# A residual tail without turns between blocks, and rows turned by transposition in place of a product with a diagonal, at the end of an attention layer

## The chip, the core and the metric

The kernel runs on one core of a Trainium2 chip. The metric is the device time of one execution in microseconds; a kernel's time is the median of its runs. The core's engines work from queues of their own, each in its program's order: TensorE (PE; its weight loads are listed as PEld), VectorE (DVE), ScalarE (ACT), GpSimd (POOL) and SyncE (SP), which here issues the transfers (DMAs).

## What is computed

The reference is one step of a two-layer decoder trunk over 1024 prompt rows and 8 x 4 sample rows of width 1024, in float32. The first layer is sliding-window attention (16 heads of 64, 4 key heads), the second a gated DeltaNet (16 value heads of 128, a short causal convolution, chunks solved one after another). In short:

```
for layer in (attention, DeltaNet):
    shift, scale, gate = split(silu(c) @ w_mod[layer] + b_mod[layer], 3)
    h = rms_norm(x, norm_g[layer]) * (1 + scale) + shift
    x = x + gate * branch(h)          # branch = (mixer(h) * silu(z)) @ w_out
y = rms_norm(x, final_norm_g)
```

The change lies where the first layer ends and the second begins: `x + gate * branch(h)` for the attention layer, and `rms_norm`, `scale` and `shift` for the DeltaNet layer.

## The kernel before

**Numbers.** A product of float32 matrices is made of three faster ones: each operand is split into a rounded part (`hi`, type fp32r) and a rest (`lo`), and hi x hi, hi x lo and lo x hi are summed in PSUM. Rows are worked in nine blocks: eight of 128 prompt rows and one of the 32 sample rows. The output projection of layer 1 takes them in the order of `turned_` (L1136), which is 0, 8, 1, 2, ..., 7. The text calls the position in this list the block's place: place 1 is the sample block (t = 8), place 8 the last full block (t = 7).

**How the order is made.** While the program is written out, the class `Core` (L96 to L175) keeps a table of assumed durations: for each engine the time at which it would be free, for each tile the time at which it would be written. Work beside the main line of matmuls stands in generators, which `weave` (L486) puts into a list sorted by a rank from the table `K` (L241). Between two matmuls of the main line, `stages` (L497) goes through the list and advances each generator as far as its condition lets it: `ready` (the tiles are written by TensorE's assumed time), `soon`, `idle` (an engine is about to be free), or a counter. So the order of every engine's queue is fixed before the kernel runs, and on the chip an instruction that is late holds up everything behind it on its engine. `until` (L508) holds the main line itself until a condition is met.

**Around the change.** The loop at L1437 takes the places 0 to 8. For each it does 48 matmuls into two PSUM banks, one for each half (512 columns, `hf`) of the output row; `opened` counts the banks that are not yet read. When a half is complete it weaves `add_out` (L1337). For a full block that is: wait for its turn; multiply the bank by `gate` into a tile `y` (VectorE), which closes the bank; add `y` to the row block `xt` (GpSimd; at place 8, second half, VectorE); square with a row sum (ScalarE). With the second half the row block is stored to `x1d` and `shape` is woven (L1376): the row sum becomes rs = 1/sqrt(mean + eps) by some 13 small VectorE steps (`rsqrt`, L196); VectorE makes `dg`, the identity times rs; for each half of the block TensorE multiplies four 128 x 128 pieces of `xt` with `dg`, which scales the rows and turns them at once; the result is scaled and shifted (ScalarE for the first half, VectorE for the second) into `fu`, and split into `h2hi` (ScalarE) and `h2lo` (VectorE). Then `shaped` goes up by one.

The turn of an addition is this condition in `add_out` (L1341), for place i and half hf:

```
yield lambda: gathered[0] == 2 * i + hf and i in rows_ and shaped[0] >= i - 1 + hf
```

that is: the additions come in order, the row block has been asked for, and so many blocks are shaped. `rows_in` (L1328) asks for the row block of place i once `shaped[0] >= i - 1`, into a ring of two tiles. `y` and `dg` share another ring of two.

**What follows.** At place 7 `first_weights` (L1420) is woven; once the gate of layer 2 is computed it loads and splits the convolution's weights `cwr` (turned into `cT`) and the first key weights `kw0`, `kw1`. Behind the projection, `run_k` (L2147) starts the first key projection of layer 2, in groups of 384, 384 and 288 rows of h2: group 0 waits until at most one bank is in `opened`, group 1 until none is (L2149). The first query projection follows with its groups 0 and 1, then the 288-wide groups of both. A group of h2 is used once 4, 7 or 9 blocks are shaped (L556). `decays` (L1502), woven too, multiplies h2 with the small weights `wab` by the same groups, and then computes the decay of each head by a long chain of VectorE and ScalarE steps; TensorE sums its result `gpr` at L1586. `projector` (L576) loads the weights of the next projections (`wr`), and splits them on ScalarE (`wh`) and GpSimd (`wl`). `conv` (L1655) copies a projection to `XR` and applies the taps of the convolution.

In the profile all operations of this part carry the line L89, that of the helper which records them, so they are told apart by the names of their tiles.

Of the kernel before, what the change touches and what calls it, by code (L numbers as in the profile page):

```python
# [5 lines left out]
F32 = mybir.dt.float32  # L6
F32R = mybir.dt.float32r
I32 = mybir.dt.int32
AF = mybir.ActivationFunctionType
# [5 lines left out]
P = 128  # L15
D = 1024
# [175 lines left out]
def f(ap):  # L192
    return ap.bitcast(F32)
# [26 lines left out]
def body(tc, I, O, cst_ap, dbg=None):  # L220
    nc = tc.nc
# [25 lines left out]
    SEQ = [(a[0], int(a[1:])) for a in """z0 z1 z2 k1 v0 q1 z3 v1 k2 q2 z4 z5 k3 v2 q3 z6 z7 k4 v3 q4 z8 z9 k5 v4 q5  # L247
        z10 z11 k6 v5 q6 z12 z13 k7 v6 q7 v7 z14 z15""".split()]
    MM = (0, 20)
    ORDER = [("q", 2), ("q", 3), ("q", 4), ("q", 5), ("z", 0), ("k", 1), ("z", 1), ("z", 2), ("q", 6), ("q", 7),  # L250
             ("z", 3), ("z", 4), ("z", 5), ("z", 6), ("z", 7)]
    SE = ("vector", "vector", "vector", "vector")
# [44 lines left out]
    ident = C["ident"]  # L297
# [220 lines left out]
    def plain():  # L518
        return not isinstance(nc, Core)

    def ready(*ts):
        return lambda: plain() or nc.ready(ts) <= nc.free["tensor"]
# [4 lines left out]
    def idle(eng, *ts):  # L527
        return lambda: plain() or max(nc.free[eng], nc.ready(ts)) <= nc.free["tensor"] + AI
# [7 lines left out]
    def bank(tag):  # L536

        q = held.setdefault(tag, [])
        yield lambda: len(q) < banks[tag] or q[-banks[tag]] is None
        t = psb(tag)  # L540
        q.append(t.tensor.name)
        yield lambda: plain() or nc.after(nc.used, t, "tensor") <= nc.free["tensor"]
        return t
# [80 lines left out]
    for t in range(NB + 1):  # L624
        parts = P if t < NB else TS
# [62 lines left out]
    def qpieces(pr, g):  # L688
        return [(64 * a, ((2 * pr + a) * 4 + g) * 64, 64) for a in range(2)]
# [73 lines left out]
    if True:  # L763
# [373 lines left out]
        split_, gathered, placed = {}, [-1], set()  # L1137
# [81 lines left out]
        for m in range(KD // 2):  # L1219
# [7 lines left out]
        plan = [(win, {"k": lambda b: [(0, 1024 + b * P, P)], "q": lambda b: qpieces(b // 4, b % 4), "z": zpieces}[a](b))  # L1227
                for a, b in ORDER]
        w_raw, w_split, projected = projector(plan)
# [3 lines left out]
        for t in range(NB + 1):  # L1233
            parts = P if t < NB else TS
            pv = psb("pj3")[0:parts, 0:256]
            n = 0
            for k in range(KD):
                hi, lo = wv[k // 2]
                for x, y in ((hhi, hi), (hlo, hi), (hhi, lo)):
                    with pinned():  # L1240
                        mm = nc.tensor.matmul(pv, x[:, k, t * P:t * P + parts], y[:, k % 2, :],
                                              start=(n == 0), stop=(n == 23))
# [7 lines left out]
        pt = psb()  # L1250
# [5 lines left out]
        def modulation_rest():  # L1256
# [12 lines left out]
            for k in range(KD):  # L1269
                yield lambda: ticks[0] >= t0 + MM[0] + MM[1] * (2 * k + 1)  # L1270
                yield ready(*wts)
# [16 lines left out]
        nc = Core(tc)  # L1288
# [8 lines left out]
        weave(keys0[0], "turning")  # L1297
        for i, (a, b) in enumerate(ORDER):
            if a == "k":
# [12 lines left out]
    if True:  # L1312
# [9 lines left out]
        x2 = Watched(nc, x2_guard.__enter__(), since=nc.free["tensor"])  # L1322
        nc.parts.add(x1d.tensor.name)
        gate = x2.tile([P, D], F32, name="gp")
        rows_, opened, outs, shaped = {}, [], [0], [0]
        kwr, kw = [], []

        def rows_in(i, t):  # L1328
            yield lambda: shaped[0] >= i - 1
            xt = rows_[i] = x2.tile([P, D], F32, tag="xt", name="xt", bufs=2)  # L1330
            nc.sync.dma_start(xt[0:P if t < NB else TS], xp_rows[t * P:(t + 1) * P] if t < NB else xs_rows)
            if t == NB:
                o, w = COFF["sels"]
                selt = rows_["sel"] = xo.tile([P, w], F32, name="sels")
                nc.sync.dma_start(selt, cst_ap[:, o:o + w])

        def add_out(pj, i, t, hf):  # L1337

            parts = P if t < NB else TS
            ns = slice(hf * 512, (hf + 1) * 512)  # L1340
            yield lambda: gathered[0] == 2 * i + hf and i in rows_ and shaped[0] >= i - 1 + hf  # L1341
            xt = rows_[i][0:parts]
            if t < NB:
                yield idle("vector", pj)
                y = x2.tile([P, 512], F32, tag="y", name="y", bufs=2)
                nc.vector.tensor_tensor(y, pj, gate[:, ns], ALU.mult)
                opened.pop(0)
            else:
                yield idle("scalar", pj)
                y = x2.tile([P, 512], F32, tag="y", name="y", bufs=2)  # L1350
                nc.scalar.copy(y[0:TS], pj[TS:2 * TS])
                yield idle("vector", y)
                nc.vector.tensor_tensor(y[0:TS], y[0:TS], pj[0:TS], ALU.add)
                opened.pop(0)
                selt = rows_["sel"]
                yield ready(selt)
                pg = yield from bank("lg")
                nc.tensor.matmul(pg[0:TS], selt[:, hf * TS:(hf + 1) * TS], modGt, start=True, stop=True)
                yield idle("vector", y, pg)
                nc.vector.tensor_tensor(y[0:TS], y[0:TS], pg[0:TS], ALU.mult)  # L1360
                give("lg", pg)
            eng = "vector" if i == NB and hf else "gpsimd"
            yield idle(eng, y, xt)
            getattr(nc, eng).tensor_tensor(xt[:, ns], xt[:, ns], y[0:parts], ALU.add)
            if hf == 0:
                rows_["ss", i] = sm.tile([P, 2], F32, tag="ss", name="ss")[0:parts]
            yield soon(xt)
            nc.scalar.activation(y[0:parts], xt[:, ns], AF.Square, accum_out=rows_["ss", i][:, hf:hf + 1])
            gathered[0] += 1
            if hf == 1:  # L1370
                nc.sync.dma_start(x1d[t * P:t * P + parts], xt)
                weave(shape(i, t, xt, rows_["ss", i], parts), "shape")
                if t == NB:
                    weave(modulation_gate(1, wp, 4, "wr"), "mod")

        def shape(i, t, xt, ss, parts):  # L1376

            nonlocal x2_guard
            yield idle("vector", ss)
            sv = sm.tile([P, 1], F32, tag="sv", name="sv")[0:parts]  # L1380
            nc.vector.tensor_tensor(sv, ss[:, 0:1], ss[:, 1:2], ALU.add)
            nc.vector.tensor_scalar(sv, sv, 1.0 / D, EPS, ALU.mult, ALU.add)
            rs = sm.tile([P, 1], F32, tag="rs", name="rs")[0:parts]
            rsqrt(nc, sm, rs, sv, 1, parts)
            dg = x2.tile([P, 512], F32, tag="y", name="dg", bufs=2)[0:parts, 0:parts]
            nc.vector.tensor_scalar_mul(dg, ident[0:parts, 0:parts], rs)
            for kk in range(2):
                yield ready(dg, xt)
                pt = yield from bank("lg")
                for q in range(4):  # L1390
                    nc.tensor.matmul(pt[:, q * parts:(q + 1) * parts], xt[:, (4 * kk + q) * P:(4 * kk + q + 1) * P], dg,
                                     start=True, stop=True)
                fu = x2.tile([P, 4, P], F32, tag="fu", name="fu", bufs=2)
                yield soon(pt, fu)
                for q in range(4):
                    k = 4 * kk + q
                    if t < NB and kk == 0:
                        nc.scalar.activation(fu[:, q, :], pt[:, q * P:(q + 1) * P], AF.Identity,
                                             bias=Sh[1][:, k, 0:1], scale=Sc[1][:, k, 0:1])
                    elif t < NB:  # L1400
                        nc.vector.tensor_scalar(fu[:, q, :], pt[:, q * P:(q + 1) * P],
                                                Sc[1][:, k, 0:1], Sh[1][:, k, 0:1], ALU.mult, ALU.add)
                    else:
                        o3 = fu[:, q, 0:TS].rearrange("p (b t) -> p b t", t=DS)
                        nc.vector.tensor_tensor(o3, pt[:, q * TS:(q + 1) * TS].rearrange("p (b t) -> p b t", t=DS),
                                                Sc[1][:, k, 1:9].unsqueeze(2).to_broadcast([P, DB, DS]), ALU.mult)
                        nc.vector.tensor_tensor(o3, o3, Sh[1][:, k, 1:9].unsqueeze(2).to_broadcast([P, DB, DS]), ALU.add)
                give("lg", pt)
                fv = fu[:, :, 0:parts]
                c0 = t * P % GW  # L1410
                hi, lo = (h[t // 3][:, 4 * kk:4 * kk + 4, c0:c0 + parts] for h in (h2hi, h2lo))
                yield idle("scalar", fu)
                nc.scalar.copy(hi, fv)
                yield idle("vector", hi)
                nc.vector.tensor_sub(lo, fv, f(hi))
            shaped[0] += 1
            if shaped[0] == NB + 1:
                x2_guard.__exit__(None, None, None)
# [18 lines left out]
        for i, t in enumerate(turned_):  # L1437
# [7 lines left out]
            for kk, hf in order if i < NB else sorted(order, key=lambda o: o[::-1]):  # L1445
                if True:
                    ns = slice(hf * 512, (hf + 1) * 512)
                    if hf not in pjs:
                        tag = ("pj", "pj", "mi", "mi")[outs[0] % 4]
# [5 lines left out]
                    for k in range(4 * kk, 4 * kk + 4):  # L1455
# [187 lines left out]
    if True:  # L1643
# [544 lines left out]
        pos, prepared, stored, opened, gathered, outs = [0], {}, [0], [], [-1], [0]  # L2188
# [485 lines left out]
    nc = nc.nc  # L2674
# [36 lines left out]
```

## Time and profile before

| | us |
|---|---|
| median of three runs | 1722.98 |
| lowest and highest run | 1719.68, 1724.67 |
| the profiled execution | 1721.68 |
| its span in the profile | 1719.9 |
| output projection of layer 1, first to last matmul of places 0 to 8, in the trace | to 535.3 |
| last row block shaped (last `h2lo`) | 569.2 to 569.9 |

Times in the trace count from the span's start. A row of a timeline has the start, the duration, engine, line, operation, output<-inputs, shape and count, and in brackets how long the engine had been idle and what it waited for. Matmuls overlap, so the distance of two starts, not the duration, says what one costs.

### The profile page before, as it was taken

Reading aid. Unit: us, or ns where it says so; the run is one execution under the profiler, and the core shown is the slowest. Engines: PE = TensorE matmul, PEld = TensorE weight load, DVE = VectorE, ACT = ScalarE, POOL = GpSimd, SP = SyncE. Lnnn points to the kernel's source line nnn. Section 1 sums busy time; section 2 is a strip of 40 time slices with the busy share of each in tenths; the row PEclk is TensorE's granted clock in tenths of the full one; section 3 lists DMA queues with packets and bytes.
Section 4 is the critical chain, followed back from the end, with each engine's and each line's share of the span. In section 5 each row is a group of like instructions: output and inputs, shape, how many; then the busy total and the mean of one; then the engine's idle time right before and its main releaser. Section 6 shows DMA issues by size and latency. Waiting matters only on the chain.

```text
span 1719.9 us, 31798 instructions
## 1 busy us (share of the span) xinstructions
PE 1629.0 (95%) x10666; PEld 1436.5 (84%) x10666; DVE 1204.6 (70%) x3538; ACT 862.6 (50%) x2514; POOL 613.4 (36%) x1170
## 2 busy tenths in 40 slices
PE   6999999998999999999899999999999998999897
PEld 5988888986777898999889899899999896767685
DVE  4526676564565578897889878788797875468677
ACT  4625565444333546475463655654656654333332
POOL 2601111112112226463453534445344455323332
PEclk9999999999999999999999999999999999999999
DMA  9542221233243142232332324224242237765885
GB/s 331 150 138 66 59 58 50 56 89 111 86 134 105 54 111 50 66 97 56 106 74 66 98 52 112 64 72 114 51 115 60 51 85 209 236 181 160 255 259 171
DMA packets 281573, 191.78 MB, mean 112 GB/s; under 512 B 98361, under 2 KB 253881, under 8 KB 281378
## 3 DMA queue, kind: packets, MB, share of 16 engines
q1 hardware_dynamic: 281410, 189.75, 38.1%
q8 instruction: 85, 1.39, 0.3%
q14 instruction: 78, 0.64, 0.1%
HBM read 144.68 MB, written 47.04 MB: 111 GB/s over the span
## 4 chain that ended last, share of the span: by engine, by line
PE 30%; DVE 8%; DMA 4%; ACT 3%; issue 2%; POOL 2%; SPq 1%; POOLq 0%; ACTq 0%; DVEq 0%
PE ps_pj L89 17%; PE ps_lg L89 4%; PE ps_mi L89 4%; PE ps_tr L89 2%; PE ps_ob L89 2%; DMA S<-in_state_gdn_s 2%; DVE vT L89 1%; DVE UZ L89 1%; DMA out_new_s_s<-S 1%; POOL rst L89 1%; DMA out_y_p<-xt 1%; DVE rst L89 1%; DVE S L89 1%; SPq L89 1%; DVE tmp L89 0%
## 5 line engine op out<-in xcount | busy, mean ns | idle before, releaser
L89 PE MATMUL ps_pj<-h2hi,wl 128*128 128x384 f32 (+1 forms) x1128 | 383.1, 340 | 2.7 <-POOL wl L89 2.7
L89 PE MATMUL ps_pj<-h2hi,wh 128*128 128x384 f32 (+1 forms) x1128 | 383.2, 340 | 2.1 <-ACT wh L89 2.1
L89 PE MATMUL ps_pj<-h2lo,wh 128*128 128x384 f32 (+1 forms) x1128 | 381.6, 338 | 0.0
L89 POOL TENSOR_TENSOR wl<-wr,wh 128x512 fp32r<-128x512 f32 x122 | 163.4, 1340 | 543.3 <-ACT wh L89 492.9
L89 PEld LDWEIGHTS ps_pj<-h2hi,wl 128*128 128x128 f32 x1128 | 216.0, 191 | 6.8 <-POOL wl L89 3.6
L89 PEld LDWEIGHTS ps_pj<-h2hi,wh 128*128 128x128 f32 x1128 | 215.9, 191 | 4.8 <-ACT wh L89 2.4
L89 PEld LDWEIGHTS ps_pj<-h2lo,wh 128*128 128x128 f32 x1128 | 215.7, 191 | 3.3
L89 POOL TENSOR_TENSOR xt<-xt,y 128x512 f32<-128x512 f32 (+1 forms) x48 | 64.0, 1337 | 173.5 <-DVE y L89 138.1
L89 PE MATMUL ps_pj<-hlo,wh 128*128 128x384 f32 (+1 forms) x360 | 119.0, 331 | 0.0
L89 PE MATMUL ps_pj<-hhi,wh 128*128 128x384 f32 (+1 forms) x360 | 118.4, 329 | 0.0
L89 PE MATMUL ps_pj<-hhi,wl 128*128 128x384 f32 (+1 forms) x360 | 117.9, 328 | 0.0
L89 DVE SCALAR_TENSOR_TENSOR vT<-XR,cT,vT 128x384 f32<-128x384 f32 (+1 forms) x144 | 90.5, 638 | 25.4 <-ACT vT L89 23.8
L89 DVE TENSOR_TENSOR X<-X,tmp 64x31 f32<-64x31 f32 (+15 forms) x248 | 95.2, 384 | 8.5
L89 DVE TENSOR_TENSOR tmp<-X 64x31 f32<-64x31 f32 (+15 forms) x248 | 93.5, 377 | 4.9 <-POOL X L89 1.7
L89 ACT CAST wh<-wr 128x512 fp32r<-128x512 f32 x122 | 75.1, 616 | 13.1 <-PE ps_pj L89 8.0
L89 PEld LDWEIGHTS ps_pj<-hlo,wh 128*128 128x128 f32 x360 | 67.7, 188 | 11.2 <-issue 11.1
L89 ACT ACTIVATE vo<-vo,fo 128x128 f32<-128x128 f32 x128 | 42.2, 392 | 59.7 <-POOL fo L89 59.7
L89 PEld LDWEIGHTS ps_pj<-hhi,wh 128*128 128x128 f32 x360 | 67.7, 188 | 2.7 <-issue 2.7
L89 ACT ACTIVATE prob<-prob,nm 128x256 f32<-128x256 f32 (+1 forms) x128 | 62.2, 489 | 14.8 <-DVE nm L89 14.6
L89 PEld LDWEIGHTS ps_pj<-hhi,wl 128*128 128x128 f32 x360 | 67.7, 188 | 2.1 <-issue 2.1
L89 POOL TENSOR_TENSOR Xd<-Xc,cst 32x128 f32<-32x128 f32 x128 | 65.7, 513 | 10.7 <-DMA Xc<-Xdd 3.1
L89 ACT ACTIVATE qe<-ps_mi,Eg 128x128 f32<-128x128 f32 x112 | 35.0, 363 | 64.4 <-PE ps_mi L89 64.4
(580 smaller groups left out, 4235.0 us busy)
## 6 DMA issues: line engine op xcount, KB each, us to landing
wr<-in_gdn_w_in SPq DMA_DIRECT2D x96, 256.0 KB
S<-in_state_gdn_s SPq DMA_DIRECT2D x40, 256.0 KB
xt<-in_x_prompt SPq DMA_DIRECT2D x16, 512.0 KB
wm<-in_w_mod SPq DMA_DIRECT2D x16, 512.0 KB
wr<-in_swa_w_in SPq DMA_DIRECT2D x64, 128.0 KB
wmod<-in_w_mod SPq DMA_DIRECT2D x32, 256.0 KB
wm<-in_w_mod SPq DMA_DIRECT2D x32, 256.0 KB
DP<-gcr SPq DMA_DIRECT2D x64, 128.0 KB
```

What stands on the lines that cost most here:

```text
L89: inst = fn(*args, **kwargs)
```

## The change

Three things are edited. In `add_out` the part of the condition that counts shaped blocks is dropped; the order of the additions, and the row block being asked for, stay. `rows_in` gets a name, XT, for the size of its ring and for the condition that goes with it; with XT = 2 it is what it was. And `shape` has a second way of turning, used at the places in TP2: it scales each half of the row block by rs into a tile `xs` of its own, the first half on VectorE, the second on ScalarE (TE2), and turns the four pieces by transpositions. TP2 holds 0 to 7, so this is done for seven full blocks and the sample block; place 8 keeps the product with `dg`, which gets a ring of its own.

```diff
+    TP2, TE2 = (0, 1, 2, 3, 4, 5, 6, 7), ('vector', 'scalar')
+    XT = 2
...
         def rows_in(i, t):
-            yield lambda: shaped[0] >= i - 1
-            xt = rows_[i] = x2.tile([P, D], F32, tag="xt", name="xt", bufs=2)
+            yield lambda: shaped[0] >= i - XT + 1
+            xt = rows_[i] = x2.tile([P, D], F32, tag="xt", name="xt", bufs=XT)
...
-            yield lambda: gathered[0] == 2 * i + hf and i in rows_ and shaped[0] >= i - 1 + hf
+            yield lambda: gathered[0] == 2 * i + hf and i in rows_
...
-            dg = x2.tile([P, 512], F32, tag="y", name="dg", bufs=2)[0:parts, 0:parts]
-            nc.vector.tensor_scalar_mul(dg, ident[0:parts, 0:parts], rs)
+            plain_ = i in TP2
+            if not plain_:
+                dg = x2.tile([P, P], F32, tag="dg", name="dg", bufs=2)[0:parts, 0:parts]
+                nc.vector.tensor_scalar_mul(dg, ident[0:parts, 0:parts], rs)
             for kk in range(2):
+                if plain_:
+                    xs = x2.tile([P, 512], F32, tag="xs", name="xs", bufs=2)[0:parts]
+                    eng = TE2[kk]
+                    yield idle(eng, rs)
+                    if eng == "scalar":
+                        nc.scalar.activation(xs, xt[:, kk * 512:(kk + 1) * 512], AF.Copy, scale=rs)
+                    else:
+                        getattr(nc, eng).tensor_scalar_mul(xs, xt[:, kk * 512:(kk + 1) * 512], rs)
+                    yield ready(xs)
+                    pt = yield from bank("lg")
+                    for q in range(4):
+                        nc.tensor.transpose(pt[:, q * parts:(q + 1) * parts], xs[:, q * P:(q + 1) * P],
+                                            ident[0:parts, 0:parts])
+                else:
...
```

More of the change, by code (lines that the diff above doesn't have):

```diff
@@ L1384, in shape @@
             rsqrt(nc, sm, rs, sv, 1, parts)
-            dg = x2.tile([P, 512], F32, tag="y", name="dg", bufs=2)[0:parts, 0:parts]
-            nc.vector.tensor_scalar_mul(dg, ident[0:parts, 0:parts], rs)
+            plain_ = i in TP2
+            if not plain_:
+                dg = x2.tile([P, P], F32, tag="dg", name="dg", bufs=2)[0:parts, 0:parts]
+                nc.vector.tensor_scalar_mul(dg, ident[0:parts, 0:parts], rs)
             for kk in range(2):
[L1388 to L1392, printed above, removed]
+                if plain_:
[12 more added lines that the diff above has]
+                else:
+                    yield ready(dg, xt)
+                    pt = yield from bank("lg")
+                    for q in range(4):
+                        nc.tensor.matmul(pt[:, q * parts:(q + 1) * parts], xt[:, (4 * kk + q) * P:(4 * kk + q + 1) * P], dg,
+                                         start=True, stop=True)
                 fu = x2.tile([P, 4, P], F32, tag="fu", name="fu", bufs=2)
```

## The prediction

> **What bounds the kernel now.** I read the page's totals, then busy time by stretches around the output projection of layer 1 (the code the change touches), then TensorE's waits there, then the timelines of TensorE, VectorE and GpSimd.
>
> ```profile
> span 1719.9 us, 31798 instructions
> PE 1629.0 (95%) x10666; PEld 1436.5 (84%) x10666; DVE 1204.6 (70%) x3538; ACT 862.6 (50%) x2514; POOL 613.4 (36%) x1170
> ```
> ```profile
> 200.00:300.00 100.00, 100.00 (x690) 86.85 (x686) 69.11 (x254) 57.87 (x190) 11.69 (x9) 1.00 0.21 57
> ...
> 430.00:530.00 100.00, 100.00 (x500) 76.99 (x499) 59.52 (x184) 36.45 (x85) 19.84 (x15) 1.00 0.32 106
> ...
> 530.00:540.00 10.00, 6.71 (x34) 4.74 (x27) 7.66 (x18) 4.41 (x9) 7.29 (x9) 0.94 0.71 190
> 540.00:550.00 10.00, 10.00 (x50) 9.33 (x50) 2.06 (x5) 2.51 (x8) 1.53 (x3) 0.72 0.34 95
> 580.00:590.00 10.00, 6.75 (x42) 6.25 (x41) 9.23 (x21) 4.22 (x10) 5.48 (x10) 1.00 0.21 55
> 590.00:600.00 10.00, 10.00 (x60) 9.82 (x59) 3.48 (x12) 5.68 (x17) 2.90 (x9) 0.83 0.42 119
> 600.00:610.00 10.00, 7.53 (x27) 6.70 (x26) 6.75 (x24) 5.36 (x20) 2.51 (x2) 0.68 0.67 177
> ```
> ```profile
> PE ps_lg L89 <- DVE gpr L89: 3.2, 1, 3.2
> PE ps_lg L89 <- DVE cT L89: 3.0, 1, 3.0
> PE ps_pj L89 <- ACT wh L89: 2.1, 1, 2.1
> PE ps_pj L89 <- ACT XR L89: 0.8, 1, 0.8
> ...
> PE ps_lg L89 <- DVE dg L89: 0.3, 1, 0.3
> ```
>
> The columns of a stretch are its length, then busy time of PE, PEld, DVE, ACT and POOL, the granted TensorE clock, the DMA share and GB/s. From 430 to 530, while the nine blocks go through the output projection, TensorE is busy 100.00 of 100.00 at clock 1.00; VectorE has 40 us free, ScalarE 64. So here TensorE's own work sets the time: whatever its queue loses is won, and work given to VectorE or ScalarE is covered. Behind 530 this ends. The waits of TensorE between 430 and 620 (waiter, releaser, total, times, longest) are four of weight, and after three of them the granted clock is below one: 0.72 in 540 to 550, 0.83 in 590 to 600, 0.68 in 600 to 610. A wait there costs its own length and then about (1 - clock) of the next 10 us.
>
> **Turning by transposition.** Now each half of a normalised block is turned by four plain matmuls of a block of rows with diag(rs).
>
> ```profile
> L89 PE MATMUL ps_lg<-dg,xt x144: 270/275/579, 438.2 to 564.6; 128*128 128x128 f32 x128, 32*128 32x32 f32 x16
> ```
> ```profile
> 467.48 0.39 PE L89 MATMUL ps_mi<-wlo,ohi 128*128 128x512 f32 x1
> 467.71 1.05 PE L89 MATMUL ps_lg<-dg,xt 128*128 128x128 f32 x8
> 468.52 0.48 PE L89 MATMUL ps_pj<-whi,ohi 128*128 128x512 f32 x1
> 468.83 0.40 PE L89 MATMUL ps_pj<-whi,olo 128*128 128x512 f32 x1
> ...
> 453.27 1.07 PE L89 MATMUL ps_lg<-dg,xt 32*128 32x32 f32 x8
> ...
> 454.61 0.40 PE L89 MATMUL ps_mi<-whi,olo 128*128 128x512 f32 x1
> ...
> 598.97 0.60 PE L89 MATMUL ps_mi<-cst,kT 128*128 128x128 f32 x4
> ...
> 599.60 0.34 PE L89 MATMUL ps_pj<-h2lo,wh 128*128 128x384 f32 x1
> 599.78 0.34 PE L89 MATMUL ps_pj<-h2hi,wl 128*128 128x384 f32 x1
> ```
>
> Nine blocks of two halves of four are 72 matmuls with 144 records: a plain float32 matmul leaves two. Starts, not durations, give the price, since matmuls overlap. From the burst at 467.71 to the second matmul behind it are 1.12 us; the one projection matmul in between takes 0.23 (467.48 to 467.71), so a burst costs 0.89. The sample block's (32 rows) costs 454.61 - 453.27 - 0.23 = 1.11. Four float32 transpositions stand in the trace as four records, at 598.97: 599.60 - 598.97 less one matmul of 0.18 is 0.45. A full half saves 0.44. The sample block's transposition by the new code has no row; it is no dearer than 0.45 and no cheaper than nothing, so it saves 0.66 to 1.11; I take 0.66.
>
> TP2 holds the places 0 to 7 in the order 0, 8, 1, ..., 7 of `turned_`: the sample block is in it, the last full block (place 8) is not and keeps the diagonal. Places 0 and 2 to 6 are turned before the projection ends: 12 halves x 0.44 + 2 x 0.66 = 6.6 us off a TensorE without a gap. Place 7 falls into the tail, where TensorE waits anyway; I count nothing for it.
>
> What it adds:
>
> ```profile
> L89 DVE TENSOR_SCALAR dg<-cst,rs x9: 228/287/1600, 436.3 to 559.6; 128x128 f32<-128x128 f32 x8, 32x32 f32<-32x32 f32 x1
> ```
> ```profile
> L89 DVE TENSOR_SCALAR prob<-prob,sm x128: 276/348/1427, 120.8 to 372.0; 128x256 f32<-128x256 f32 x112, 128x128 f32<-128x128 f32 x16
> ```
> ```profile
> L89 ACT ACTIVATE y<-xt x18: 622/632/643, 430.8 to 556.1; 128x512 f32<-128x512 f32 x16, 32x512 f32<-32x512 f32 x2
> ```
> ```profile
> 474.72 0.69 DVE L89 TENSOR_TENSOR h2lo<-fu,h2hi 128x512 fp32r<-128x512 f32 x1 [0.69 <-ACT h2hi L89]
> 475.33 0.68 DVE L89 TENSOR_TENSOR y<-ps_mi,gp 128x512 f32<-128x512 f32 x1
> ```
>
> VectorE scales a 128x512 half in place of making a 128x128 diagonal. The same operation took 0.29 at 128 columns and 0.35 at 256, 0.06 more; carried on that is 0.47 at 512, and the 0.68 of a two-operand 512 bounds it above: 0.2 to 0.4 more, eight times, at most 3.2 us of 40 free. ScalarE gets eight new 128x512 scalings, 0.63 each by its square of that size: 5.1 us of 64 free. Both cost the end nothing while TensorE is full. Uncovered (a row split `ohi` queued behind a scaling in ScalarE's order, with TensorE waiting for it) a scaling would cost up to 0.63, all eight 5.1.
>
> In front of this row a rule speaks against the edit. The Trainium skill, "TensorE: Matmul & The Clock Gate", Part 4, gives about 275 ns for a transposition in a kernel, and says that transpose mode does not count as busy for the clock. By that price four would take 1.1 us, an estimate from the page. The trace agrees with the duration of a record (0.60 for four overlapped) but not with adding them; and 200 to 300, where attention turns its probabilities by transposition all the time, kept clock 1.00.
>
> **The looser turns.** `add_out` waited for `shaped[0] >= i - 1 + hf`. For the first half `rows_in` still asks for the same number (XT is 2), so nothing changes. For the second half the wait for the shaping of the block before goes. Block place 3 shows it: TensorE had finished at 467.7 (the row 467.48 is its last), and its second addition began at 475.33, right behind the last step of the block before at 474.72. Inside the full stretch that costs nothing. At the end it does:
>
> ```profile
> 535.08 0.39 PE L89 MATMUL ps_pj<-wlo,ohi 128*128 128x512 f32 x1
> ```
> ```profile
> 534.88 1.18 DVE L89 SCALAR_TENSOR_TENSOR rst<-rst,sv 128x1 f32<-128x1 f32 x1
> 536.10 1.19 DVE L89 SCALAR_TENSOR_TENSOR rsw<-rst,rsw 128x1 f32<-128x1 f32 x1
> ...
> 537.91 1.60 DVE L89 TENSOR_SCALAR dg<-cst,rs 128x128 f32<-128x128 f32 x1
> ...
> 553.96 0.69 DVE L89 TENSOR_TENSOR h2lo<-fu,h2hi 128x512 fp32r<-128x512 f32 x1 [5.72 <-ACT h2hi L89]
> 554.57 0.68 DVE L89 TENSOR_TENSOR y<-ps_pj,gp 128x512 f32<-128x512 f32 x1
> ```
> ```profile
> 534.76 1.29 POOL L89 TENSOR_TENSOR kw0l<-wr,kw0h 128x512 fp32r<-128x512 f32 x1 [1.27 <-ACT kw0h L89]
> ...
> 539.39 1.26 POOL L89 TENSOR_TENSOR wl<-wr,wh 128x512 fp32r<-128x512 f32 x1
> ```
>
> The projection ends at 535.3, but the last block's second half is gated only at 554.57, 19 us later, behind the shaping of place 7. That addition does more than close the block: `run_k` lets the second group of the first key projection start only when no output bank is open, and this one stays open until 554.57. In those 19 us TensorE runs what little it is given and loses 3.0 (behind a VectorE held up three times by about 1 us while GpSimd splits weights), 0.8 (XR), and by the clock 10 x 0.28 = 2.8: 6.6 us.
>
> After the change the last gating follows the projection's end at once. What moves with it: its gate, add and norm on VectorE, its square on ScalarE, its 512 KB store on SP, and the turn on TensorE. They come forward past the first taps on VectorE and, on SP, up to the weight loads; at 190 GB/s the store is 2.8 us of transfers. The query weights' last split ended at 540.65, 5.4 us behind the projection; with the bank free TensorE wants them after two key groups, 48 x 0.18 = 8.6 us behind it. The margin of 3.2 covers the store, just. And the last block's norm now falls beside GpSimd's weight splits, where place 7's was. So the next thing to be late is the last block's diagonal: between the 0.3 that it waited in its old place (DVE dg, 0.3) and place 7's 3.0 + 2.8. It is near neither; I take the middle, 3.1. The tail gains 6.6 - 3.1 = 3.5; bounds 0.8 to 6.3.
>
> Behind it stand the 3.2 for gpr and the 2.1 for wh. The gpr chain starts earlier, but TensorE's place for it is planned from a table of durations and the chain runs late against it wherever it stands; I leave both.
>
> **Sum.** The profiled execution took 1721.68 us, 1.78 of it outside the span. 6.6 + 3.5 = 10.1 off gives 1711.6; the median of the runs is 1.3 above the profiled one: 1713.
>
> **Rivals.**
> 1. More of the tail goes (0.15). Decays that start some 15 us earlier, on a VectorE with only 2.06 of 10 us busy at 540 to 550, finish before TensorE asks: gpr's 3.2 and its 1.7 of clock go, and the remaining 3.1: 1705. Against: the planned order.
> 2. The tail keeps its hole in another place (0.22). The last diagonal is held as place 7's was (2.7 more), and the query weights come late by the store (2.8): 1713 + 5.5 = 1718.5.
> 3. Slower (0.12), by one mechanism: norm steps on VectorE meeting GpSimd's splits. Earlier norms, taps and decays crowd into the stretch of those splits, and each one late enough to stop TensorE costs 3.0 + 2.8 = 5.8. Two would leave about 1725; from the third it is slower: 1713 + 17.4 = 1730. For: three steps of 1.2 to 1.6 above. Against: only one such hole in this stretch before. The Trainium skill, "SBUF — State Buffer", Who interferes with whom, has it that a VectorE instruction with two SBUF inputs contends with a GpSimd one that reads SBUF; the 1.18 and 1.19 beside 534.76 agree.
> 4. The looser turn finds nothing to loosen (0.13), something else holding the last addition: only the bursts count, 1713 + 3.5 = 1716.5.
> 5. Transpositions that don't overlap (0.03): at 0.27 each, the shortest record of the row x144, a burst takes 1.1 in place of 0.89 and adds 0.2 to each of 14 halves; 6.6 saved turns into 2.9 lost: 1722.5. Against: four in 0.45 at 598.97. The Trainium skill's price, above, is of this kind.
>
> My forecast has 0.35.
>
> **Numbers.** A measurement of this kernel can tell about 0.3%, 5.2 us, from no change: faster is below 1717.8, slower above 1728.2. Faster: the forecast, rival 1, most of 4, a little of 2: 0.60. Same: most of 2, the rest of 4, nearly all of 5: 0.27. Slower: rival 3 and a tail of the others: 0.13. The range reaches 3 us past rival 1, about its remaining wait for wh, and up to 3.4 past two holes of rival 3, short of the third: 1702 to 1728.
>
> **What would show it.** Right: bursts of 0.45 us; places 0 to 6 done with the projection ending near 528.7; the second addition of each block within 2 us of its last matmul; the last gating before 532; TensorE from there to the first 288-wide key matmul without a wait over 2 us. Wrong: the projection's end not earlier by 6 us (bursts, or TensorE waiting for `ohi`), the last gating still 10 us late, or the saved time given back behind 620, where nothing is edited but the planned order can differ.

## The result, and the profile after

The changed kernel takes 1704.99 us (median of 4 runs, 1701.84 to 1708.93); beside it the kernel before took 1721.39 (1719.68 to 1724.67). The ratio is 0.9908, interval 0.9888 to 0.9928: faster by 16 us, 6 more than the 10.1 of the sum. The profiled execution took 1701.84. Its totals:

```profile
span 1700.1 us, 31684 instructions
PE 1612.1 (95%) x10602; PEld 1418.3 (83%) x10602; DVE 1207.6 (71%) x3538; ACT 866.1 (51%) x2522; POOL 611.4 (36%) x1170
```

TensorE has 64 matmul records fewer (16 halves of four, one record in place of two) and 16.9 us less busy time. The stretches (length, then PE, PEld, DVE, ACT and POOL, the granted clock, DMA share, GB/s):

```profile
430.00:530.00 100.00, 99.72 (x474) 75.18 (x473) 65.27 (x203) 45.61 (x104) 24.36 (x21) 1.00 0.39 123
530.00:540.00 10.00, 9.05 (x54) 7.47 (x54) 8.01 (x22) 3.30 (x9) 3.52 (x5) 1.00 0.50 142
540.00:550.00 10.00, 10.00 (x68) 9.96 (x67) 5.52 (x10) 6.86 (x13) 1.64 (x1) 1.00 0.00 0
570.00:580.00 10.00, 7.39 (x35) 7.07 (x35) 4.35 (x14) 4.43 (x14) 4.57 (x11) 0.83 0.52 150
600.00:610.00 10.00, 10.00 (x66) 10.00 (x65) 5.99 (x25) 1.52 (x4) 4.06 (x13) 1.00 0.56 150
```

Behind the projection TensorE is busy for 9.05 and 10.00 of 10 us at clock 1.00, where before it had 6.71 and then 10.00 at a clock of 0.72. Its waits from 400 to 620 (waiter, releaser, total, times, longest):

```profile
PE ps_lg L89 <- DVE gbs L89: 2.6, 1, 2.6
PE ps_lg L89 <- issue: 2.1, 1, 2.1
...
PE ps_lg L89 <- ACT xs L89: 0.9, 1, 0.9
...
PE ps_lg L89 <- DVE gpr L89: 0.9, 1, 0.9
```

The waits for cT (3.0) and wh (2.1) are gone. The wait for gpr is 0.9 in place of 3.2, but a later step of the same decays, gbs, is waited for 2.6, with a clock of 0.83 about it (570 to 580): the two together are 3.5. TensorE's rows: one burst, the end of the projection, then the tail:

```profile
466.43 0.39 PE L89 MATMUL ps_pj<-whi,ohi 128*128 128x512 f32 x1
466.66 0.60 PE L89 MATMUL ps_lg<-cst,xs 128*128 128x128 f32 x4
467.01 0.48 PE L89 MATMUL ps_pj<-whi,olo 128*128 128x512 f32 x1
467.33 0.40 PE L89 MATMUL ps_pj<-wlo,ohi 128*128 128x512 f32 x1
```
```profile
526.55 0.39 PE L89 MATMUL ps_pj<-wlo,ohi 128*128 128x512 f32 x1
526.77 0.33 PE L89 MATMUL ps_pj<-h2hi,kw0h 128*128 128x384 f32 x1
...
533.24 0.66 PE L89 MATMUL ps_lg<-cst,xs 128*128 128x128 f32 x4 [0.95 <-ACT xs L89]
...
540.16 1.05 PE L89 MATMUL ps_lg<-dg,xt 128*128 128x128 f32 x8
...
557.46 0.29 PE L89 MATMUL ps_pj<-h2hi,kw0h 128*128 128x288 f32 x1
```

A burst costs 467.33 - 466.66 - 0.23 = 0.44. VectorE in the tail, and the scalings (the group of a line: form, times, then busy time and mean ns):

```profile
526.97 0.69 DVE L89 TENSOR_TENSOR y<-ps_pj,gp 128x512 f32<-128x512 f32 x1 [2.45 <-PE ps_pj L89]
529.91 1.64 DVE L89 TENSOR_TENSOR h2lo<-fu,h2hi 128x512 fp32r<-128x512 f32 x1 [1.52 <-ACT h2hi L89]
531.47 1.24 DVE L89 TENSOR_TENSOR sv<-ss 128x1 f32<-128x1 f32 x1
```
```profile
L89 ACT ACTIVATE xs<-xt,rs 128x512 f32<-128x512 f32 x7 | 5.0, 721 | 0.0
L89 DVE TENSOR_SCALAR xs<-xt,rs 128x512 f32<-128x512 f32 x7 | 3.3, 478 | 0.0
```

The last gating stands 0.42 us behind the last matmul's start; before, it stood 19.5 behind.

**Four stretches.** To see where time goes, each profile is cut by rows of TensorE: A, the output projection's first to last matmul; B, from there to the first 288-wide key matmul (557.46 above); C, from there to the first matmul of the fifth later projection of layer 2 (the fifth that uses `wh`, 632.90 before and 611.26 after); D, the rest of the span. The change edits nothing behind C's start, and in all kernels below the operations of D are the same; their planned order can differ. Between the two profiled executions: A 117.95 to 111.73 (-6.2), B 38.89 to 30.91 (-8.0), C 58.93 to 53.80 (-5.1), D 1086.95 to 1088.79 (+1.8). The projection also began 2.3 earlier (414.82 against 417.13), with nothing edited before it: the two executions differ by that much ahead of the change. These five add up to the 19.8 between the spans.

| kernel | median, us | ratio to before | A | B | C | D |
|---|---|---|---|---|---|---|
| before | 1721.39 | | 117.95 | 38.89 | 58.93 | 1086.95 |
| after | 1704.99 | 0.9908 [0.9888, 0.9928] | 111.73 | 30.91 | 53.80 | 1088.79 |
| e1_loose | 1718.43 | 0.9994 [0.9980, 1.0007] | 119.83 | 29.26 | 52.16 | 1101.11 |
| e2_turned | 1736.63 | 1.0098 [1.0075, 1.0121] | 113.23 | 50.75 | 54.04 | 1098.53 |
| e3_last | 1730.35 | 1.0064 [1.0046, 1.0082] | 113.41 | 37.39 | 58.44 | 1098.92 |
| e4_bank | 1706.66 | 0.9926 [0.9909, 0.9944] | 111.09 | 28.38 | 60.76 | 1089.24 |
| e6_twice | 1717.41 | 0.9970 [0.9955, 0.9986] | 117.47 | 30.30 | 53.80 | 1095.71 |
| e7_after_plan | 1716.77 | 0.9975 [0.9958, 0.9991] | 113.57 | 31.32 | 55.26 | 1101.43 |
| e8_loose_plan | 1723.36 | 1.0009 [0.9995, 1.0023] | 119.82 | 29.27 | 53.51 | 1097.83 |
| e9_before_plan | 1719.38 | 0.9992 [0.9973, 1.0011] | 117.88 | 36.37 | 55.87 | 1088.61 |
| e5_nine | 1733.42 | 1.0083 [1.0069, 1.0098] | 111.56 | 31.07 | 52.41 | 1117.97 |
| e10_after_plan3 | 1713.07 | 0.9966 [0.9954, 0.9977] | 111.64 | 30.42 | 57.41 | 1093.64 |
| e11_before_plan3 | 1730.11 | 1.0062 [1.0048, 1.0077] | 117.93 | 36.39 | 56.67 | 1099.94 |
| e12_after_planm | 1706.14 | 0.9930 [0.9915, 0.9946] | 112.07 | 31.09 | 53.13 | 1090.74 |

Each ratio is to runs of the kernel before on the same chip and in the same batch, whose medians were 1719.95 (e1 to e4), 1721.11 (e6 to e9) and 1718.37 (the last four). Each stretch is of one profiled execution, and that isn't always a typical one: those of e1 and e7 are the slowest of their twelve runs, about 7 us above the median. Part of this lies ahead of A, where nothing is edited: A begins anywhere from 414.8 (after) to 421.7 (e6).

### The profile page after: what moved, and what is told of

Read it like the earlier page. It is cut to its first block, busy times and chain, and to the rows that moved or that the text cites. A ratio compares the mean times of both kernels' runs of the same rounds, so it can differ in the third digit from the quotient of the medians.

```text
span 1700.1 us, 31684 instructions
## 1 busy us (share of the span) xinstructions
PE 1612.1 (95%) x10602; PEld 1418.3 (83%) x10602; DVE 1207.6 (71%) x3538; ACT 866.1 (51%) x2522; POOL 611.4 (36%) x1170
## 5 line engine op out<-in xcount | busy, mean ns | idle before, releaser
L89 PE MATMUL ps_pj<-h2hi,wl 128*128 128x384 f32 (+1 forms) x1128 | 379.1, 336 | 2.0 <-POOL wl L89 2.0
L89 PE MATMUL ps_pj<-hhi,wl 128*128 128x384 f32 (+1 forms) x360 | 117.9, 328 | 0.0
L89 DVE TENSOR_TENSOR X<-X,tmp 64x31 f32<-64x31 f32 (+15 forms) x248 | 99.8, 402 | 8.5
L89 POOL TENSOR_TENSOR Xd<-Xc,cst 32x128 f32<-32x128 f32 x128 | 64.0, 500 | 22.5 <-DMA Xc<-Xdd 13.2
```

What stands on the lines that cost most here:

```text
L89: inst = fn(*args, **kwargs)
```

## The experiments

The theory was at first that of the prediction: two separate gains, one for each edit, with the bank that closes early behind the second. The rivals: the transpositions alone make the difference; what counts is the early shaping of the last block and not the bank; the planned order does it.

**One edit alone.** e1_loose is the kernel before with the looser condition; e2_turned is the changed kernel with the old one.

```diff
# e1_loose, in before
-            yield lambda: gathered[0] == 2 * i + hf and i in rows_ and shaped[0] >= i - 1 + hf
+            yield lambda: gathered[0] == 2 * i + hf and i in rows_
# e2_turned, in after
-            yield lambda: gathered[0] == 2 * i + hf and i in rows_
+            yield lambda: gathered[0] == 2 * i + hf and i in rows_ and shaped[0] >= i - 1 + hf
```

> The kernel before with one edit: add_out's condition loses its part about shaped blocks; all nine blocks are still turned by products with dg. Theory (two separate gains: bursts while TensorE is full, and the last output bank closed at once): the projection ends where it did, the last gating moves from 554.6 to about 536, and the 288-wide key group starts about 8 us earlier: some 8 us off in all, 1713. Rival A (the transpositions do it all, the looser turn finds nothing): within 2 us of before.

> The changed kernel with the old condition in add_out: only the way of turning differs from before. Theory: the projection ends 6 to 7 us earlier, and the tail keeps its waits: 6 to 7 us off, 1714 to 1715. Rival A (transpositions do it all): the whole 16 us off, 1705.

Both missed. e1 is level with before, where the theory had 8 off; e2 is slower than before by 1.0%, where it had 6 off. The stretches take them apart. In e1 the 288-wide key group does start 7.75 us earlier, counted from A's start, as expected. By the end of C e1 has won 14.5 us, and it loses 14.2 in D, where nothing is edited. e2's loss lies in B, 50.75 against 30.91. Its VectorE, one block (place 3), and its TensorE:

```profile
465.37 0.68 DVE L89 TENSOR_TENSOR y<-ps_pj,gp 128x512 f32<-128x512 f32 x1
...
481.46 0.69 DVE L89 TENSOR_TENSOR h2lo<-fu,h2hi 128x512 fp32r<-128x512 f32 x1 [0.69 <-ACT h2hi L89]
482.07 0.68 DVE L89 TENSOR_TENSOR y<-ps_mi,gp 128x512 f32<-128x512 f32 x1
```
```profile
467.71 0.39 PE L89 MATMUL ps_mi<-wlo,ohi 128*128 128x512 f32 x1
...
480.84 0.39 PE L89 MATMUL ps_pj<-wlo,ohi 128*128 128x512 f32 x1
```

465.37 is the second gating of place 2 and 482.07 that of place 3. Between them lies the whole chain of a block: gate, add, square, norm, scale, turn, shift, split, and only then the next gate. It takes 16.7 us there. TensorE's last matmuls of places 3 and 4 are 13.1 apart. So the blocks fall behind. The distance from a place's last matmul to its second gating is 10.9, 14.4, 15.9, 18.5, 18.0, 29.4 and 30.2 in e2, for the places 2 to 8. In the kernel before it stays at 7.3 to 8.5 from place 2 to 7, because there the chain (475.33 - 460.37 = 15.0 at place 3, 13.3 to 13.9 at the places 4 to 7) and TensorE (13.6, the mean over five places from 452.95 to 520.91) have nearly the same period. Over the places 3 to 6 both have moved in e2: TensorE's period from 13.8 to 13.2, and that of the chain, which now has the scalings in it, from 13.9 to 15.0. What the delay costs at the end of e2's projection:

```profile
532.83 0.39 PE L89 MATMUL ps_pj<-wlo,ohi 128*128 128x512 f32 x1
538.26 1.10 PE L89 MATMUL ps_lg<-cst,xs 128*128 128x128 f32 x4 [5.04 <-DVE xs L89]
...
550.81 0.37 PE L89 MATMUL ps_pj<-h2hi,kw0h 128*128 128x384 f32 x1
```
```profile
532.79 1.14 DVE L89 SCALAR_TENSOR_TENSOR rsw<-rst,rsw 128x1 f32<-128x1 f32 x1
533.96 1.19 DVE L89 TENSOR_TENSOR rst<-rsw 128x1 f32<-128x1 f32 x1
535.18 1.26 DVE L89 SCALAR_TENSOR_TENSOR rst<-rst,sv 128x1 f32<-128x1 f32 x1
...
536.75 1.45 DVE L89 TENSOR_SCALAR xs<-xt,rs 128x512 f32<-128x512 f32 x1
...
550.01 0.68 DVE L89 TENSOR_TENSOR y<-ps_pj,gp 128x512 f32<-128x512 f32 x1
```
```profile
532.64 1.28 POOL L89 TENSOR_TENSOR kw0l<-wr,kw0h 128x512 fp32r<-128x512 f32 x1 [1.43 <-ACT kw0h L89]
533.87 1.26 POOL L89 TENSOR_TENSOR kw1l<-wr,kw1h 128x512 fp32r<-128x512 f32 x1
...
535.16 1.26 POOL L89 TENSOR_TENSOR wl<-wr,wh 128x512 fp32r<-128x512 f32 x1
...
536.66 1.26 POOL L89 TENSOR_TENSOR wl<-wr,wh 128x512 fp32r<-128x512 f32 x1
```

The first key matmul, which follows the projection at once in the changed kernel, comes 18 us after it here: the first bank of place 8 is only gated at 550.01. TensorE is not idle for all of it: it does the matmuls with `wab` first. On the way place 6's norm meets four weight splits on GpSimd: three small steps take 1.14 to 1.26, and the scaling 1.45 in place of 0.48. TensorE waits 5.04 for it. This is rival 3's mechanism, and in the changed kernel it doesn't stop TensorE in the tail. But the kernel before pays for such a meeting too, at place 7's norm, and there the distance at place 8 is 19.5. What e2 has more, 30.2 against 19.5, is the delay that the turns had gathered.

**Only the last turn free, or only the bank.** e3_last keeps the old condition at all places but 8; e4_bank keeps the wait at every full block, but behind the gating, so that only the closing of the bank is loosened.

```diff
# e3_last, in after
-            yield lambda: gathered[0] == 2 * i + hf and i in rows_
+            yield lambda: gathered[0] == 2 * i + hf and i in rows_ and (i == NB or shaped[0] >= i - 1 + hf)
...
# e4_bank, in after
                 nc.vector.tensor_tensor(y, pj, gate[:, ns], ALU.mult)
                 opened.pop(0)
+                yield lambda: shaped[0] >= i - 1 + hf
```

> The changed kernel with the old condition at places 0 to 7; only the last block's two additions are free of it. Theory: the places before never mattered, since TensorE is full there; the last bank is closed at once, so it is as fast as the changed kernel, 16 us off within 4. Rival B (the gain comes from all blocks being shaped earlier, so that decays and taps start earlier): only the bursts and a small part of the tail, 7 to 9 us off.

> The changed kernel with the old wait moved behind the gating in full blocks: the output bank is closed at once, but the addition, the square, the norm and the turn wait for the block before to be shaped, as in the old code. Theory (the bank is what the tail waits for): the second key group starts right behind the first, and most of the gain is there, 13 to 16 us off. Rival B (earlier shaping is what counts): the bursts alone, 6 to 8 us off.

NB is 8, so `i == NB` is the last place. e3 went against the theory: 1730.35, 25 above the changed kernel. D has 10 of them; A to C are 209.2, 12.8 longer than after's 196.4. Loosening the last turn alone isn't enough: additions still come in order, and place 8 stands behind a place 7 that is 29 us late. e4 has the bank in time and the shaping late. VectorE in e4:

```profile
531.09 0.67 DVE L89 TENSOR_TENSOR y<-ps_pj,gp 128x512 f32<-128x512 f32 x1
...
546.31 0.16 DVE L89 TENSOR_TENSOR sv<-ss 128x1 f32<-128x1 f32 x1 [1.15 <-ACT y L89]
...
558.97 0.68 DVE L89 TENSOR_TENSOR h2lo<-fu,h2hi 128x512 fp32r<-128x512 f32 x1
```

531.09 is the last gating, 2.4 us after the projection; the norm of the last block begins at 546.31 (531.47 in the changed kernel) and its last split at 558.97 (548.20). Yet the median is 1706.66, 13 below before in the same batch, as the theory had it. B is 28.4, but it ends early here, because 16 matmuls with `wab` stand behind the first key matmul of 288 columns and not ahead of it:

```profile
557.07 0.29 PE L89 MATMUL ps_pj<-h2hi,kw0h 128*128 128x288 f32 x1
...
560.68 0.29 PE L89 MATMUL ps_pj<-h2lo,kw0h 128*128 128x288 f32 x1
```

Counted to the second such matmul it is 32.0, against 31.0 in the changed kernel and 39.1 before. In it are two waits for the late block, 0.55 for h2hi and 0.40 for h2lo. So the tail waited for the output bank; the late shaping costs about 1 us there. C is 7 longer than after's, and 3 longer than in any other profile of the changed kernel. Some 3.5 of the 7 are the `wab` matmuls and the two waits, and gpr is waited for 3.3 again in place of 0.9: the late block delays the decays.

**The size of a transposition.** e6_twice turns each half twice.

```diff
-                    for q in range(4):
+                    for q in (0, 1, 2, 3) * 2:
                         nc.tensor.transpose(pt[:, q * parts:(q + 1) * parts], xs[:, q * P:(q + 1) * P],
```

> The changed kernel with each turn by transposition made twice into the same bank: eight transpositions in place of four, in 16 halves; the rest is the same. Theory (TensorE is full there, and with the looser turn its own work sets the pace): each half costs TensorE four more transpositions, 0.36 to 0.45 us, so the projection ends 5 to 6 us later than in the changed kernel and the whole is 5 to 7 us slower than it. Rival (the pace is set by the chain of turns, not by TensorE): no later end of the projection, within 2 us of the changed kernel.

```profile
449.98 1.03 PE L89 MATMUL ps_lg<-cst,xs 128*128 128x128 f32 x8
450.77 0.48 PE L89 MATMUL ps_pj<-whi,ohi 128*128 128x512 f32 x1
451.08 0.40 PE L89 MATMUL ps_pj<-whi,olo 128*128 128x512 f32 x1
```

The end of the projection came as the theory had it: A is 5.7 us longer than in the changed kernel. Eight cost 451.08 - 449.98 - 0.23 = 0.87, four 0.44. B and C are after's to 0.6. The total missed: the median rose by 12 us, where 5 to 7 were expected. In the profiled execution D is 6.9 longer.

**The planned order.** The runs so far had the same operations take 1087 to 1101 us in D. So the planner's assumed time of TensorE was moved once, ahead of the chunk stage; no operation is edited. TensorE's order changes from within C on (from 566 us in the changed kernel, from 582 in the kernel before).

```diff
+        nc.free["tensor"] += 1.0        # e7 in after, e8 in e1_loose, e9 in before; 3.0: e10 in after, e11 in before; -1.0: e12 in after
         for kind, i in SEQ:
```

> The changed kernel; where the list of layer-2 projections begins, 1 us is added to TensorE's assumed clock in the table of durations, so that the same operations behind it are put into another order. Theory (the planned order behind the tail is worth several us either way, by luck): unchanged up to that point, and up to 8 us off the changed kernel at the end, either way. Rival (what stands behind the tail runs the same whatever the order): within 2 us of it.

> The kernel before with the looser condition alone, and 1 us added to the assumed clock in the same place. With the looser condition alone, 14 us were won up to the fifth projection of layer 2 and lost again behind it. Theory (lost by the luck of the order): another order keeps a part of them, 1705 to 1715. Rival (what stands behind is bound by something that did not move, so that any early start is given back): 1717 to 1721, as without.

> The kernel before, with 1 us added to the assumed clock in the same place; nothing else. Theory (luck of the order): up to 10 us off the kernel before, more likely slower if its order is a good one. Rival (the order is worth little): within 2 us of it.

e7 is 12 us above the changed kernel, past the 8 that the theory allowed; its profiled execution has 12.6 more in D. e8 missed, at 1723.36 above both its values: e1's loss in D isn't one unlucky order, for a second order has it too (1097.8). e9 didn't move. Then, with place 8 turned by transposition as well in e5_nine:

```diff
-    TP2, TE2 = (0, 1, 2, 3, 4, 5, 6, 7), ('vector', 'scalar')
+    TP2, TE2 = (0, 1, 2, 3, 4, 5, 6, 7, 8), ('vector', 'scalar')
```

> The changed kernel with place 8 turned by transposition too (TP2 holds 0 to 8). Theory (the last turn is off the bottleneck: in the changed kernel its diagonal was used at 540.16 without a wait, behind key group 1): two bursts of eight records less, 2 x 0.44 = 0.9 us of TensorE work, but the last block's second scaling (0.7) stands on ScalarE in the stretch of the weight splits; first matmul of the projection to the fifth projection of layer 2 within 1 us of the changed kernel's 196.4. The total differs by at most 12 us either way through the planned order behind that, where nothing is edited. Rival (the last block's turn is on the path): that stretch 2 us or more shorter or longer.

> The changed kernel with the planner's assumed time of TensorE moved later by 3.0 us ahead of the chunk stage; no operation is edited. Theory (about 196 to 201 us from the first matmul of the projection to the fifth projection of layer 2 are the edits' own; what comes behind depends on the planned order by 0 to 14 us, and the changed kernel as handed over has a good order): 1705 to 1718, so faster than before by 2 to 15. Rival (1705 is the usual level of the changed kernel, and the 1.0 us nudge met a bad order): within 3 us of 1705.

> The kernel before with the same 3.0 us. Theory (its order, too, is one of many): within 8 us of 1721 either way. Rival (the order of before is an unlucky one and most others are better): 1713 or less.

> The changed kernel with the planner's assumed time of TensorE moved earlier by 1.0 us at the same place. Theory: 1705 to 1718, as for 3.0 later; rival: within 3 us of 1705. With the two others the mean of four planned orders of the changed kernel, and of three of the kernel before, says what the edits are worth apart from the order.

e5 is the plainest. Its A to C are 195.0, 1.4 less than after's, where within 1 was expected and 2 would have been the rival's; but its D is 1118, and the median is 28 us above the changed kernel's, where 12 had been the bound. Its totals:

```profile
span 1731.7 us, 31620 instructions
...
PE 1622.6 (94%) x10594; PEld 1422.5 (82%) x10594; DVE 1216.3 (70%) x3538; ACT 867.1 (50%) x2523; POOL 610.9 (35%) x1170
```

With 8 matmul records fewer, TensorE is idle for 109.1 us (88.0 in the changed kernel) and busy for 10.5 more. From 620 on its longest wait behind any one releaser sums to 10.6, so this is no single hole but many small ones.

Which orders are new shows when TensorE's rows in D are laid side by side, by tile and shape. e12 differs from the changed kernel in 8 of some 6700 rows, and e9 from the kernel before in 18. So e12 and e9 have nearly the old orders, and their times are nearly the old times (1706.14, 1719.38); the expectation of e12 counted it as an order of its own, which was wrong. e7, e10 and e5 differ from the changed kernel in 2914, 2972 and 3260 rows, and e11 from the kernel before in 2986; e7 and e10 differ from each other in 878. The new orders came with slower medians: by 12 (e7), 8 (e10, as expected), 28 (e5), and 9 (e11; 12 against the kernel before in its own batch), where the theory allowed 8.

The order isn't all of it, though. e1 has the changed kernel's rows in D but for 8, and e6 too; yet their D is 1101.1 and 1095.7, against 1088.8 and 1090.7 (e12). e8 has e7's rows but for 10, with 1097.8 against 1101.4. So four kernels of one order lie up to 12.3 apart in D (by one profiled execution each, e1's a slow one), about as far as most of the new orders lie from the old. The medians agree that it isn't the order alone: e6's rose by 7 us more than its A to C. e1 keeps the order of the changed kernel and still loses 12.3 against it: 6.2 of that is more idle time of TensorE (53.9 against 47.6), in small waits of which none grew by more than 1.4. That the order alone is worth over 10 us is shown for neither kernel; only e5 lies far outside what one order gave.

**What the edits are worth.** A to C of the three profiles of before (before, e9, e11) average 117.9, 37.2 and 57.2; of the four of the changed kernel (after, e7, e10, e12) 112.3, 30.9 and 54.9. That is 5.7 + 6.3 + 2.3 = 14.2 us (rounded terms), and the single sums of A to C don't overlap (196.3 to 200.2 against 210.1 to 215.8). D averages 1091.8 before and 1093.7 after: no gain of the edits shows there. A and B are clear (142.1 to 144.9 together against 154.3 to 156.8); C alone is not, for its values overlap (53.1 to 57.4 against 55.9 to 58.9), and in the nudged kernels a part of it has another order. So 12 us of the 14.2 are firm. The medians say about the same, 1711.6 as the mean of about 1705, 1713 and 1717 against 1725 as that of about 1720 and 1730, though with so few kernels that difference is uncertain by several us.

A and B together give the four corners: 155.1 before, 149.1 with the looser turn alone (e1, e8), 164.0 with the transpositions alone (e2), 143.2 with both. Alone, the looser turn wins 6.0 and the transpositions lose 8.9; together they win 11.9.

## Why the prediction was right, and where not

The forecast was 1713.0 in 1702 to 1728, with 0.6 on faster; 1704.99 lies inside, and it is faster by more than 0.3%. The two mechanisms of the sum are there, but the step that kept them apart was wrong, and that the total came out 6 us better than the sum rests in part on luck in D.

**Bursts, 6.6 us off the projection.** Measured: 0.44 a burst, A shorter by 6.2 in the profiled execution and 5.7 on average. The term that was mis-sized is "place 7's counted at nothing": in the kernel before both its halves were turned behind the projection (32 records of `dg,xt` in B), now the first stands inside it (4 records of `xs` and 16 of `dg` in B). So A carries 0.45 more than counted, 6.6 - 0.45 = 6.15, and B 2 x 0.89 - 0.45 = 1.3 less. The sample block's burst cost 452.15 - 451.46 - 0.23 = 0.46, so the 0.66 taken for its saving was right. Rival 5, a burst at the full record length, falls with e6: four more transpositions in each of the 15 halves inside A made it 5.7 longer. By the price in the Trainium skill, "TensorE: Matmul & The Clock Gate", Part 4, they would have cost some 16 us, an estimate from that page.

**Scalings hidden.** Right for the changed kernel: VectorE's cost 0.48 each (0.47 forecast), ScalarE's 0.72 (0.63), and A didn't lose them; one in the tail held TensorE for 0.95. They aren't hidden where the turns remain: in e2 they stand in the chain, whose period is 1.1 longer there. That the scalings are all of this 1.1 is not shown.

**"Inside the full stretch that costs nothing."** This step failed. It was read from TensorE's 100.00 of 100.00, and for the kernel before it is true: releasing the turn alone left A no shorter (e1's 119.8 is longer by the 2 x 0.89 of place 7, now inside). But the constant 7.3 to 8.5 between a place's end and its gating meant that the chain of turns had TensorE's own period. A faster TensorE runs away from it, and the scalings make the chain slower still. e2 shows what then comes: 18 us from the projection's end to the first key matmul. The looser turn isn't only a gain of the tail; it is what lets the transpositions count. Because both edits came together, this error cost the forecast's number nothing; the prediction doesn't say that one edit needs the other. Rival 4, nothing to loosen, is refuted by the same run and by e1's B (29.3 against 37.2).

**The tail, 3.5 us.** The mechanism was right: the last bank closes at once, and e4 shows that the bank, and hardly the shaping, is what the tail waited for. The size was low: B gave 8.0 in the profiled execution, 6.3 on average. Of that 1.3 are place 7's bursts, and some 5 the stall. Two terms were off. The 6.6 of losses were one execution's: with the same order ahead of it, e9 waits 1.7 where the kernel before waited 3.0, and loses less clock:

```profile
PE ps_lg L89 <- DVE dg L89: 2.0, 2, 1.7
```
```profile
530.00:540.00 10.00, 8.02 (x37) 6.53 (x38) 6.45 (x17) 5.53 (x13) 7.17 (x9) 0.93 0.80 217
540.00:550.00 10.00, 10.00 (x57) 8.72 (x56) 2.06 (x5) 2.07 (x8) 1.19 (x3) 0.90 0.24 68
```

And the 3.1 kept for the last diagonal didn't come. The first step of its norm did meet a split on GpSimd, as rival 3 has it (1.24 at 531.47 in VectorE's rows above, where the later steps took about 0.16; place 7's `h2lo` took 1.64 at 529.91). The Trainium skill, "SBUF — State Buffer", Who interferes with whom, has it that a VectorE instruction with two SBUF inputs contends with a GpSimd one that reads SBUF; both rows have two inputs, and a split runs on GpSimd beside each (from 529.72 and 531.23), so the trace agrees. But the diagonal was made by 535.4, and with the bank closed TensorE had key group 1 and the matmuls with `wab` to run; it took the diagonal at 540.16 without a wait. Rivals 2 and 3 gave TensorE too little other work in that stretch.

**gpr and wh, left at 3.2 and 2.1.** The wait for wh went. Of the decays' wait only the name changed: 0.9 for gpr and 2.6 for gbs are 3.5 in place of 3.2 (2.4, 4.4 and 1.6 for gbs in e7, e10 and e12). Rival 1 named 1705, the time that was measured, but its mechanism, that the decays finish before TensorE asks, didn't come: its number was met by luck. C gained 2.3 on average, 5.1 in the two profiled executions.

**"The saved time given back behind 620."** It was named as what would make the forecast wrong and given no price. It is the largest unknown of this kernel: D ran from 1087 to 1118 over the fourteen profiles. Against the mean of 1711.6 the forecast of 1713.0 is close, with 14 us from the edits where it counted 10; the 1705 measured holds some 7 us that D gave by luck, and e12, with nearly the same order, has them too (1706.14). What makes D long is open: e5 points at the order, e1 and e6 show that it also varies within one order.

**What would show it right.** Bursts of 0.45, a last gating before 532 (526.97) and no TensorE wait above 2 up to the first 288-wide matmul (0.95) all came. The projection ended at 526.8, where 528.7 had been named; 2.3 of that is the earlier start. The second addition came within 2 us of each place's end except at places 1 (5.1) and 6 (2.75).

## What to carry to other kernels

When an engine is full and a chain beside it keeps a constant distance, compare their periods before making the engine faster: if they are equal, the chain is the next bound, and it must be loosened together with the work that is saved. Where a program's order is planned from assumed times, compare the edited stretch by its own rows, and measure several planned orders before believing a difference of one per cent in the total; lay the orders side by side before blaming them. A buffer that stays open because its reader waits in turn can stop work that has nothing to do with the turn; here closing it early brought nearly all of the tail's gain, with the work behind it still late.

## What the runs showed of the hardware

Four more transpositions of 128 x 128 in a burst cost 0.43 us (0.87 less 0.44), about 0.11 each, against a record of 0.275. ScalarE needs 0.72 us to scale a 128 x 512 half by a value for each row, more than the 0.63 of its square with a row sum. After waits of 5.04 and 2.38 us in e2 (the burst between them took 1.10 in place of 0.60), TensorE ran a stretch at about half its pace (start to start of the same kind of matmul):

```profile
541.73 0.58 PE L89 MATMUL ps_lg<-h2hi,wab 128*64 128x384 f32 x1 [2.38 <-POOL wab L89]
542.11 0.52 PE L89 MATMUL ps_lg<-h2lo,wab 128*64 128x384 f32 x1
542.43 0.52 PE L89 MATMUL ps_lg<-h2hi,wab 128*64 128x384 f32 x1
...
545.41 0.34 PE L89 MATMUL ps_lg<-h2hi,wab 128*64 128x384 f32 x1
545.59 0.34 PE L89 MATMUL ps_lg<-h2lo,wab 128*64 128x384 f32 x1
```

It is 0.32 at first and 0.18 from 545.4 on, so the slow stretch lasts over 3 us behind the second wait. The price differs from hole to hole. By the granted clock from 540 to 550, the kernel before lost 10 x 0.28 = 2.8 us behind its wait of 3.01, and e9 10 x 0.10 = 1.0 behind its wait of 1.70 (clocks 0.72 and 0.90).
